# Mixing stage of a hybrid decoder layer: VectorE order, place of the state products, held output tiles, order of the gate products

## The chip, the cores and the metric

The kernel runs on one core of one Trainium2 chip. The metric is the device time of one execution in microseconds (us). The engines are named as in the profile: PE (TensorE), DVE (VectorE), ACT (ScalarE), POOL (GpSimd) and SP (SyncE, which here only issues DMAs); each runs its own instructions in the order of the program, and waits for the others through semaphores.

## The reference

One decoder layer on x of 512 tokens by 1024 channels, in float32: a SwiGLU, a mixing stage, a second SwiGLU, each between RMS norms and with a residual.

```
x = x + 0.5 * post1(swiglu1(pre1(x)))                  # 1024 -> 2*2816 -> 1024
h = pre2(x); q, k, v, u = split(h @ w_mix_in)           # 4 x 512 columns
a = dilated_attention(q, k, v)                          # 8 heads x 64, 3 branches merged: one softmax with a bias
s = s5(u)                                               # 32 groups x 16 channels, 64 complex states, scan over time
s = gelu(s); s = s * sigmoid(s @ w_glu + b_glu)         # 512 x 512
x = x + post2(concat(a, s) @ w_mix_out)                 # 1024 x 1024
x = x + 0.5 * post3(swiglu2(pre3(x)))
```

## The kernel before

Every float32 product is three matmuls on values split in two parts (`mm3`, L129: high by high, high by low, low by high). A weight chunk comes by DMA from SP's queue into `wraw` (one of 3 buffers), ACT casts its high part (`whi`, L102) and DVE or POOL subtracts it from the chunk for the low part (`wlo`, L104). All eight PSUM banks rotate through one pool: the next tile takes a bank whose last reader is done.

`start` (from L216) fetches x and the first weight chunks in four cuts and runs the first two chunks of the first SwiGLU as the cuts arrive; all these DMAs but that of the small parameters (`sw`) are issued by SP.

The stage that the change is about is `mix` (from L843). PE's order in it is written out by hand at its end; `f(n)` advances a generator of filling work by n pieces (`pieces`: half projections of q and k chunks, `prj`, and pieces of the value projection, `prv`), `go(n)` advances the scan on DVE by n steps (`sx`, `Hs`, L1111), and `fg` does both. The order is:

- projection 0 of q, with the late part of the norm hooked in after k-tiles 3 and 7 (`late`); four products `o0` were begun before and are multiplied by the norm into `uT`, go to DRAM (`ud`, L904) and come back in another layout as `um` (L906).
- projection 4 and half of 1, scores of head pair 0, `f(2)`: the rest of 1 and the first half of 5, then `states` (64 matmuls `st` that read `um`; ACT copies the result to `Hs` and `ends`), then the other half of 5, which makes kT of pair 1.
- transposes `pt` of pair 0's probabilities, the value projection with scan steps beside it, scores of pair 1, values `pv` of pair 0, and so on for pairs 1 to 3. Between them lie parts of the output projection (`mo`): `parts` with k-tiles 0 and 1 of several output tiles, each of which holds a PSUM bank until its k-tile 3 is done (12 matmuls for two held tiles before the scores of pair 3).
- the scan's outputs `ys`, the gelu (`ge`, `zg`, split into `zz`), the gate products `gl` of the GLU (48 matmuls: k-tiles 0 to 2 of each of four tiles m, then k-tile 3 of each), output tiles 6 and 7, and the tail of the output projection (`yt`, in the next boundary), which reads the gated result `so`.

`attn_probs` turns one head's scores into probabilities in these steps: for four row blocks, DVE adds the bias and takes the row's extreme (`nm`, L805), ACT takes the Exp with a row sum `den` (L807); then `rd` = 1/`den`, and the four blocks are scaled by it. For pair 0 both last steps are on DVE (L810, L816); for pairs 1 to 3 the reciprocal is a `pow` on POOL (L812) and the scaling on ACT (L818). Instructions given to `fix` keep the order of the program among themselves; others are placed by the scheduler. L805 is not fixed, the scan and the `prj` readers are.

Of the kernel before, what the change touches and what calls it, by code (L numbers as in the profile page):

```python
# [12 lines left out]
ALU = mybir.AluOpType  # L13
# [4 lines left out]
P = 128  # L18
# [22 lines left out]
class Layer:  # L41
# [170 lines left out]
    def start(self, chunks, ipre):  # L212


        nc = self.nc
        self.x = self.ktiles("x")  # L216
        xt = self.a["xT"].rearrange("(k p) t -> p k t", p=P)
        self.xh, self.xl = self.ktiles("xh", F32R), self.ktiles("xl", F32R)
        acc = self.acct()
        cuts = (0, 1, 3, 5, KD)  # L220
        w = [self.wtiles(KD * P) for _ in chunks[:2]]
        nc.sync.dma_start(out=self.x(0), in_=xt[:, 0])
        sw = self.sw
        for a, b in zip(cuts, cuts[1:]):
            for i, t in enumerate(w):
                if a or i:
                    nc.sync.dma_start(out=t[0][:, a * P:b * P], in_=chunks[i][:, a * P:b * P])
                if a and i == 0:
                    nc.sync.dma_start(out=self.x(a), in_=xt[:, a])
            for k in range(a + 1, b):  # L230
                nc.sync.dma_start(out=self.x(k), in_=xt[:, k])
        v = lambda t: t.rearrange("p (k m) -> p k m", m=P)
        o = [self.bank("first") for _ in w]
        for k in range(KD):
            fx = lambda: self.split(self.xh(k), self.xl(k), self.x(k), sw[:, 8 * ipre + k:8 * ipre + k + 1], fix=self.fix)
            if k == 0:
                self.fix(nc.vector.tensor_copy(out=w[0][1][:, :P], in_=sw[:, 52:]))
                fx()
                self.fix(nc.vector.tensor_tensor(out=w[0][2][:, :P], in0=sw[:, 52:],
                                                 in1=w[0][1][:, :P].bitcast(F32), op=ALU.subtract))  # L240
                self.wsplit(*(u[:, :P] for u in w[1]), fix=self.fix)
            else:
                if k in cuts:
                    sl = slice(k * P, cuts[cuts.index(k) + 1] * P)
                    for t in w:
                        self.wsplit(*(u[:, sl] for u in t), fix=self.fix)
                fx()
            for i, (_, hi, lo) in enumerate(w):
                self.mm3(o[i], v(hi)[:, k], v(lo)[:, k], self.xh(k), self.xl(k), k == 0, k == KD - 1)
        self.fix(nc.vector.tensor_copy(out=self.sm, in_=sw[:, :52]))  # L250
        nc.vector.tensor_scalar_mul(self.gh, self.sm, 0.5)
        self.ahead = [self.load(c, (KD, P)) for c in chunks[2:]]
        for k in range(KD):
            self.sq_acc(acc, self.x(k), k == 0, fix=self.fix)
        r4, r = self.rtiles()
        return o, r4, r, self.rstd(acc, r4, r)
# [540 lines left out]
    def attn_probs(self, ap, hp, i, order, place):  # L797
        nc = self.nc
        bias = ap.tile([P, S], F32, name="bias", tag="bias", bufs=2)
        nc.sync.dma_start(out=bias, in_=self.a["bias"][2 * hp + i])  # L800
        sc = ap.tile([P, 1280], F32, name="sc", tag="sc", bufs=2)
        nm, den, rd = (ap.tile([P, 4], F32, name=n, tag=n, bufs=2) for n in ("nm", "den", "rd"))
        for t in order:
            so = sc[:, QOFF[t]:QOFF[t + 1]]
            nc.vector.tensor_tensor_reduce(out=so, in0=place[t], in1=bias[:, 384 - t * P:], scale=1.0,  # L805
                                           scalar=3e38, op0=ALU.add, op1=ALU.min, accum_out=nm[:, t:t + 1])
            nc.scalar.activation(out=so, in_=so, func=AF.Exp, bias=nm[:, t:t + 1], scale=-1.0,  # L807
                                 accum_out=den[:, t:t + 1])
        if hp < 1:
            nc.vector.reciprocal(out=rd, in_=den)  # L810
        else:
            nc.gpsimd.tensor_tensor(out=rd, in0=den, in1=self.mone, op=ALU.pow)  # L812
        for t in range(4):
            so = sc[:, QOFF[t]:QOFF[t + 1]]
            if hp < 1:
                nc.vector.tensor_scalar_mul(so, so, rd[:, t:t + 1])  # L816
            else:
                nc.scalar.activation(out=so, in_=so, func=AF.Copy, scale=rd[:, t:t + 1])  # L818
        return sc
# [26 lines left out]
    def mix(self, first, scope):  # L846
# [3 lines left out]
        nc, a, tc = self.nc, self.a, self.tc  # L850
        dr = self.dr
        xh, xl = self.xh, self.xl
        o0, r4, r, late = first
        ud = dr.tile([4, P, T, NCH], F32, name="ud")

        def proj(c, hooks={}, w=None):

            w = w or self.load(a["wmi"][c], (KD, P))
            o = self.bank("prj")
            for k in range(KD):  # L860
                self.mm3(o, w[0][:, k], w[1][:, k], xh(k), xl(k), k == 0, k == KD - 1)
                if k in hooks:
                    hooks[k]()
                if k == 3 and not hooks:
                    yield
            t = pr[c] = ap.tile([P, S], F32, name="qkT"[c // 4] + "T", tag="qk", bufs=4)
            if c < 4:
                self.fix(nc.vector.scalar_tensor_tensor(out=t, in0=o, scalar=-0.125, in1=r, op0=ALU.mult, op1=ALU.mult))
            else:
                self.fix(nc.vector.tensor_tensor(out=t, in0=o, in1=r, op=ALU.mult))  # L870
            yield
# [20 lines left out]
        for j in range(T):  # L892
            nc.sync.dma_start(out=M[j * 32:(j + 1) * 32, :, j * 32:],
                              in_=self.kd[:, :, :T - j].rearrange("p n d c -> p n (d c)"))
        for _ in proj(0, {3: late[0], 7: late[1]}):
            pass
        w4 = self.load(a["wmi"][4], (KD, P))
        for m in range(4):
# [3 lines left out]
                                    in0=o0[m].rearrange("p (s i j) -> p s i j", j=T, s=SC),  # L902
                                    in1=r.rearrange("p (s i j) -> p s i j", j=T, s=SC), op=ALU.mult)
# [59 lines left out]
        def out_attn(m, ks=range(4)):  # L963

            need(m)
            if m not in mo:
                mo[m] = self.bank("mo")
            o, (wh, wl) = mo[m], wm[m // 2]
            for k in ks:
                i = 4 * (m % 2) + k  # L970
                self.mm3(o, wh[:, i], wl[:, i], cat[:, k], cat[:, 4 + k], k == 0, k == 3)
            if 3 in ks:
                nc.scalar.copy(out=y(m), in_=o)
# [11 lines left out]
        f = lambda n=1: [next(fill, None) for _ in range(n)]  # L985
# [12 lines left out]
        f()  # L998
        sc = scores(0)()
        vn = ap.tile([P, 4, S], F32, name="vn", tag="vn", bufs=1)  # L1000
        f(2)
        for n4 in range(0, NP, 4):
            states(n4)
        f()
        pt = [turn(sc[0]), turn(sc[1])]
        cat = self.b16("cat", F32R)
        scan = self.scan(sx, Hs, ends)
# [1 line left out]
        def go(n=1):  # L1009
            for _ in range(n):  # L1010
                next(scan, None)

        def fg(*n):
            for i in n:
                f()
                go(i)

        def parts(*mk):
            for m, ks in mk:
                out_attn(m, ks)  # L1020
# [8 lines left out]
        pt = [turn(sc[0])]  # L1029
        fg(1)  # L1030
        pt.append(turn(sc[1]))
        fg(1, 2)
        low = values(1, pt)
        go(2)
        low()
        sc = scores(2)()
        fg(2, 1, 1, 1)
        pt = [turn(sc[0]), turn(sc[1])]
        y = self.ktiles("ymix")
        parts((0, (0, 1)), (1, (0, 1)))  # L1040
        go()
        sc = scores(3)
        low = values(2, pt)
        sc = sc()
        go()
        low()
        parts((2, (0, 1)), (3, (0, 1)))
        go()
        parts((0, (2,)), (1, (2,)))
        pt = [turn(sc[0])]  # L1050
        go()
        parts((2, (2,)), (3, (2,)))
        pt.append(turn(sc[1]))
        go()
        out_attn(4, (0, 1))
        low = values(3, pt)
        early.close()
# [6 lines left out]
        zt = self.b16("zz", F32R)  # L1064
        go(9)
        low()
        parts((4, (2,)), (5, range(3)))
        parts(*((m, (3,)) for m in range(6)))
        wg = [[v[:, 4 * m:4 * m + 4] for v in w] for w in (self.load(a["wgl"][m2], (8, P)) for m2 in range(2))
              for m in range(2)]  # L1070
        need(6)
# [9 lines left out]
        so = [st[:, :4], st[:, 4:]]  # L1081
# [3 lines left out]
        def glu(m, ks=range(4)):  # L1085
            if m not in og:
                og[m] = self.bank("gl")
            for k in ks:
                self.mm3(og[m], wg[m][0][:, k], wg[m][1][:, k], zt[:, k], zt[:, 4 + k], k == 0, k == 3)
            if 3 in ks:  # L1090
                t = self.tmp("gt")
                nc.scalar.activation(out=t, in_=og[m], func=AF.Tanh, scale=0.25, bias=self.gh[:, 48 + m:49 + m])
                t2 = self.tmp("go")
                nc.vector.scalar_tensor_tensor(out=t2, in0=t, scalar=1.0, in1=zg[:, m], op0=ALU.add, op1=ALU.mult)
                self.split(so[0][:, m], so[1][:, m], t2, 0.25)

        for m in range(4):
            glu(m, range(3))
        for m in range(4):
            glu(m, (3,))  # L1100
        for m in range(6, KD):
            out_attn(m)
        return y, lambda i: (so[0][:, i], so[1][:, i])
# [137 lines left out]
```

## Time and profile before

| | us |
|---|---|
| median of 3 runs (lowest, highest) | 965.92 (965.55, 967.3) |
| time of the profiled execution | 967.41 |
| its span in the trace | 965.6 |
| PE busy in the span | 944.0 |
| DVE, ACT, POOL busy | 523.9, 372.4, 228.0 |

The granted PE clock averages 0.994 over the profiled span, where 1.00 is 2.4 GHz and 0.50 is 1.2 GHz. Times in the trace count from the start of the span, in us. A matmul of 512 columns shows a duration of 0.39 us, but the next begins 0.227 us after it, since they are pipelined: 12 of them stand in the chain with 2.77 us. The mixing stage lies at about 396 to 564 us. In a view of time a group "x12" is 12 neighbours, and the bracket at the end of a row says how long the engine idled before it and which instruction released it.

### The profile page before, as it was taken

Reading aid. Unit: us, or ns where it says so; the run is one execution under the profiler, and the core shown is the slowest. Engines: PE = TensorE matmul, PEld = TensorE weight load, DVE = VectorE, ACT = ScalarE, POOL = GpSimd, SP = SyncE. Lnnn points to the kernel's source line nnn. Section 1 sums busy time; section 2 is a strip of 40 time slices with the busy share of each in tenths; the row PEclk is TensorE's granted clock in tenths of the full one; section 3 lists DMA queues with packets and bytes.
Section 4 is the critical chain, followed back from the end, with each engine's and each line's share of the span. In section 5 each row is a group of like instructions: output and inputs, shape, how many; then the busy total and the mean of one; then the engine's idle time right before and its main releaser. Section 6 shows DMA issues by size and latency. Waiting matters only on the chain.

```text
span 965.6 us, 12881 instructions
## 1 busy us (share of the span) xinstructions
PE 944.0 (98%) x5082; PEld 789.4 (82%) x5082; DVE 523.9 (54%) x924; ACT 372.4 (39%) x618; POOL 228.0 (24%) x136
## 2 busy tenths in 40 slices
PE   9999999999999999999998999999999999999995
PEld 7888888888888889978766799888888888888884
DVE  7997214453256437667786568655134524444427
ACT  7353324442233224454655554543232312232312
POOL 0334212322133133400000025421122212222300
PEclk9999999999999999999999999999999999999998
DMA  8233333353334240480422430322323223234202
GB/s 264 96 101 115 102 111 129 112 190 93 117 99 144 58 161 24 147 229 23 131 66 76 152 123 1 109 88 88 101 97 109 88 88 109 91 106 131 87 1 88
DMA packets 38173, 102.48 MB, mean 106 GB/s; under 512 B 7616, under 2 KB 10944, under 8 KB 37568
## 3 DMA queue, kind: packets, MB, share of 16 engines
q1 hardware_dynamic: 37104, 98.54, 31.7%
q10 hardware_dynamic: 1008, 3.11, 0.9%
q8 instruction: 40, 0.66, 0.3%
q14 instruction: 21, 0.17, 0.1%
HBM read 94.03 MB, written 7.60 MB: 105 GB/s over the span
## 4 chain that ended last, share of the span: by engine, by line
PE 85%; DVE 6%; ACT 4%; DMA 2%; issue 2%; POOL 1%; SPq 0%; POOLq 0%; ACTq 0%; DVEq 0%
PE gu L129 46%; PE yo L129 20%; PE first L129 6%; PE yt L129 5%; PE prj L129 2%; PE st L129 1%; DVE Hs L1111 1%; PE ys L129 1%; ACT sc L818 1%; DVE sx L1111 1%; DMA um<-ud 1%; ACT sc L807 1%; PE mo L129 1%; ACT whi L102 1%; DVE wlo L104 1%
## 5 line engine op out<-in xcount | busy, mean ns | idle before, releaser
L104 POOL TENSOR_TENSOR wlo<-wraw,whi 128x1024 fp32r<-128x1024 f32 (+2 forms) x62 | 159.0, 2564 | 500.0 <-ACT whi L102 492.5
L102 ACT CAST whi<-wraw 128x1024 fp32r<-128x1024 f32 (+5 forms) x157 | 154.6, 990 | 306.0 <-PE gu L129 123.9
L129 PE MATMUL gu<-xh,whi 128*128 128x512 f32 x656 | 257.6, 393 | 0.0
L129 PE MATMUL gu<-xh,wlo 128*128 128x512 f32 x656 | 255.7, 390 | 0.5 <-DVE wlo L104 0.5
L129 PE MATMUL gu<-xl,whi 128*128 128x512 f32 x656 | 255.3, 389 | 0.0
L104 DVE TENSOR_TENSOR wlo<-wraw,whi 128x1024 fp32r<-128x1024 f32 (+5 forms) x95 | 114.0, 1203 | 122.4 <-ACT whi L102 121.7
L129 PEld LDWEIGHTS gu<-xh,wlo 128*128 128x128 f32 x656 | 123.1, 188 | 26.8 <-DVE wlo L104 1.0
L129 PEld LDWEIGHTS gu<-xh,whi 128*128 128x128 f32 x656 | 123.2, 188 | 25.3 <-issue 0.4
L129 PEld LDWEIGHTS gu<-xl,whi 128*128 128x128 f32 x656 | 123.2, 188 | 25.1
L402 DVE TENSOR_TENSOR ut<-gu,rs 128x512 f32<-128x512 f32 x41 | 28.3, 689 | 103.9 <-PE gu L129 103.8
L149 DVE TENSOR_TENSOR al<-ut,ah 128x512 fp32r<-128x512 f32 x44 | 68.5, 1560 | 24.7 <-ACT ah L148 24.7
L400 DVE TENSOR_TENSOR gt<-gu,rs 128x512 f32<-128x512 f32 x41 | 28.2, 689 | 51.8 <-PE gu L129 51.7
L129 PE MATMUL yo<-ah,whi 128*128 128x512 f32 x144 | 56.0, 389 | 0.0
L129 PE MATMUL yo<-al,whi 128*128 128x512 f32 x144 | 56.0, 389 | 0.0
L129 PE MATMUL yo<-whi,ah 128*128 128x512 f32 x144 | 56.0, 389 | 0.0
L129 PE MATMUL yo<-wlo,ah 128*128 128x512 f32 x144 | 56.0, 389 | 0.0
L129 PE MATMUL yo<-whi,al 128*128 128x512 f32 x144 | 56.0, 389 | 0.0
L129 PE MATMUL yo<-ah,wlo 128*128 128x512 f32 x144 | 56.0, 389 | 0.0
L148 ACT CAST ah<-ut 128x512 fp32r<-128x512 f32 x44 | 27.2, 621 | 61.1 <-DVE ut L403 61.1
L129 PE MATMUL first<-xh,whi 128*128 128x256 f32 (+1 forms) x144 | 43.4, 301 | 0.8 <-ACT xh L151 0.8
L129 PE MATMUL first<-xl,whi 128*128 128x256 f32 (+1 forms) x144 | 42.7, 296 | 0.3 <-DVE xl L152 0.3
L129 PE MATMUL first<-xh,wlo 128*128 128x256 f32 (+1 forms) x144 | 42.4, 295 | 0.0
(194 smaller groups left out, 1408.6 us busy)
## 6 DMA issues: line engine op xcount, KB each, us to landing
wraw<-w2i SPq DMA_DIRECT2D x44, 512.0 KB, 3.5
wraw<-w1i SPq DMA_DIRECT2D x42, 512.0 KB, 3.5
wraw<-w2o SPq DMA_DIRECT2D x18, 512.0 KB, 3.5
wraw<-w1o SPq DMA_DIRECT2D x16, 448.0 KB, 3.4
wraw<-wmi SPq DMA_DIRECT2D x12, 512.0 KB, 3.5
x<-xT SPq DMA_DIRECT2D x8, 256.0 KB, 4.6
w1d<-w1s SPq DMA_DIRECT2D x8, 256.0 KB, 2.7
w2d<-zb SPq DMA_DIRECT2D x2, 1024.0 KB, 4.9
```

The lines of the kernel that those rows point to most:

```text
L102: fix(self.nc.scalar.copy(out=hi, in_=raw))
L104: fix(eng.tensor_tensor(out=lo, in0=raw, in1=hi.bitcast(F32), op=ALU.subtract))
L129: i = self.nc.tensor.matmul(*a, **k)
L148: fix(nc.scalar.copy(out=hi, in_=src))
L149: fix(nc.vector.tensor_tensor(out=lo, in0=src, in1=hi.bitcast(F32), op=ALU.subtract))
L400: nc.vector.tensor_tensor(out=gt, in0=o[f][0], in1=r, op=ALU.mult)
L402: nc.vector.tensor_tensor(out=ut, in0=o[f][1], in1=r, op=ALU.mult)
L807: nc.scalar.activation(out=so, in_=so, func=AF.Exp, bias=nm[:, t:t + 1], scale=-1.0, accum_out=den[:, t:t + 1])
L818: nc.scalar.activation(out=so, in_=so, func=AF.Copy, scale=rd[:, t:t + 1])
L1111: tt = lambda o, x, y, op: self.fix(V.tensor_tensor(out=o, in0=x, in1=y, op=op))
```

## The change

The start: the four DMAs of the second weight chunk go to ACT's queue. In the mixing stage: (1) the norm's late part hangs on k-tiles 1 and 4 of projection 0; (2) both halves of projection 5 come ahead of the state products; (3) L805 is fixed in program order; (4) pair 2's reciprocal and scaling move from POOL and ACT to DVE; (5) before the scores of pair 3, k-tiles 0 and 1 of one output tile are computed (6 matmuls) where two were (12); tiles 1 to 3 follow the values of pair 2; (6) k-tiles 2 and 3 of output tile 5 move from before the scan's outputs to behind the gate products; (7) the gate products run k-tile by k-tile over all four tiles, with a bank for each. Scan steps (`go`) are dealt out differently between the pieces.

```diff
@@ start
-                    nc.sync.dma_start(out=t[0][:, a * P:b * P], in_=chunks[i][:, a * P:b * P])
+                    (nc.scalar if i else nc.sync).dma_start(out=t[0][:, a * P:b * P], in_=chunks[i][:, a * P:b * P])
@@ attn_probs
-            nc.vector.tensor_tensor_reduce(out=so, in0=place[t], ...
+            self.fix(nc.vector.tensor_tensor_reduce(out=so, in0=place[t], ...
-        if hp < 1:
+        if hp % 2 == 0:
             nc.vector.reciprocal(out=rd, in_=den)
...
-            if hp < 1:
+            if hp % 2 == 0:
                 nc.vector.tensor_scalar_mul(so, so, rd[:, t:t + 1])
@@ mix
-        for _ in proj(0, {3: late[0], 7: late[1]}):
+        for _ in proj(0, {1: late[0], 4: late[1]}):
...
-        f(2)
+        f(3)
         for n4 in range(0, NP, 4):
             states(n4)
-        f()
         pt = [turn(sc[0]), turn(sc[1])]
...
-        fg(1, 2)
+        fg(4, 3)
         low = values(1, pt)
-        go(2)
+        go()
         low()
         sc = scores(2)()
-        fg(2, 1, 1, 1)
+        fg(1, 1, 1, 1)
         pt = [turn(sc[0]), turn(sc[1])]
         y = self.ktiles("ymix")
-        parts((0, (0, 1)), (1, (0, 1)))
-        go()
+        out_attn(0, (0, 1))
         sc = scores(3)
         low = values(2, pt)
         sc = sc()
         go()
         low()
-        parts((2, (0, 1)), (3, (0, 1)))
+        parts((1, (0, 1)), (2, (0, 1)), (3, (0, 1)))
...
-        parts((4, (2,)), (5, range(3)))
-        parts(*((m, (3,)) for m in range(6)))
+        parts((4, (2,)), (5, (0, 1)))
+        parts(*((m, (3,)) for m in range(5)))
...
-        for m in range(4):
-            glu(m, range(3))
-        for m in range(4):
-            glu(m, (3,))
+        for k in range(4):
+            for m in range(4):
+                glu(m, (k,))
+        out_attn(5, (2, 3))
```

In the printed orders the line numbers of the changed kernel lie one or two off those of before. PE around the state products (`prj` is projection 5, `st` the states), before:

```order
L129 MATMUL prj<-xl,whi 128x512
L129 MATMUL prj<-xh,wlo 128x512
L129 MATMUL st<-um,w_3541 128x128 x32
L129 MATMUL prj<-xh,whi 128x512
L129 MATMUL prj<-xl,whi 128x512
```

And in the changed kernel (`pt` are pair 0's transposes, `prv` the value projection):

```order
L129 MATMUL prj<-xl,whi 128x512
L129 MATMUL prj<-xh,wlo 128x512
L129 MATMUL st<-um,w_3541 128x128 x32
L832 MATMUL pt<-ident,sc 128x128 x20
L129 MATMUL prv<-whi,xh 128x512
```

The second half of projection 5 (12 matmuls) has moved from behind the states to ahead of them.

PE around the scores of pair 3 (`sc`) and the values of pair 2 (`pv`), before:

```order
L129 MATMUL mo<-cat,whi 128x512 x2
L129 MATMUL mo<-cat,wlo 128x512
L129 MATMUL mo<-cat,whi 128x512 x2
L129 MATMUL mo<-cat,wlo 128x512
L129 MATMUL sc<-kT,qT 128x512 x2
L129 MATMUL sc<-kT,qT 128x128 x2
L129 MATMUL sc<-kT,qT 128x384 x2
L129 MATMUL sc<-kT,qT 128x256 x2
L129 MATMUL pv<-ptt,vn 64x512 x2
```

And in the changed kernel, from the transposes of pair 2 on:

```order
L832 MATMUL pt<-ident,sc 128x128 x20
L129 MATMUL mo<-cat,whi 128x512 x2
L129 MATMUL mo<-cat,wlo 128x512
L129 MATMUL mo<-cat,whi 128x512 x2
L129 MATMUL mo<-cat,wlo 128x512
L129 MATMUL sc<-kT,qT 128x512 x2
L129 MATMUL sc<-kT,qT 128x128 x2
L129 MATMUL sc<-kT,qT 128x384 x2
L129 MATMUL sc<-kT,qT 128x256 x2
L129 MATMUL pv<-ptt,vn 64x512 x2
```

Half of the `mo` matmuls between the transposes and the scores are gone from there; `pv` still follows the scores directly.

DVE between the readers of pair 3's q and k projections (`qT`, `kT`; `sx` and `Hs` are scan steps), before:

```order
L868 SCALAR_TENSOR_TENSOR qT<-prj,rs 128x512
L1111 TENSOR_TENSOR sx<-pw,Hs 128x480 x2
L1111 TENSOR_TENSOR Hs<-Hs,sx 128x4x120
L104 TENSOR_TENSOR wlo<-wraw,whi 128x1024
L1111 TENSOR_TENSOR Hs<-Hs,sx 128x4x120
L1111 TENSOR_TENSOR sx<-pw,Hs 128x480 x2
L1111 TENSOR_TENSOR Hs<-Hs,sx 128x4x120 x2
L870 TENSOR_TENSOR kT<-prj,rs 128x512
```

And in the changed kernel, from the scaling (L817) of pair 2's second head on, which stands behind that `qT`:

```order
L811 RECIPROCAL rd<-den 128x4
L1109 TENSOR_TENSOR Hs<-Hs,sx 128x4x120
L817 TENSOR_SCALAR sc<-sc,rd 128x128
L817 TENSOR_SCALAR sc<-sc,rd 128x256
L817 TENSOR_SCALAR sc<-sc,rd 128x384
L817 TENSOR_SCALAR sc<-sc,rd 128x512
L1109 TENSOR_TENSOR Hs<-Hs,sx 128x4x120
L1109 TENSOR_TENSOR sx<-pw,Hs 128x480 x2
L1109 TENSOR_TENSOR Hs<-Hs,sx 128x4x120
L104 TENSOR_TENSOR wlo<-wraw,whi 128x1024
L1109 TENSOR_TENSOR Hs<-Hs,sx 128x4x120
L871 TENSOR_TENSOR kT<-prj,rs 128x512
```

The reciprocals and scalings of both heads of pair 2 now stand in DVE's queue ahead of `kT`.

## Rows read from the trace of the kernel before

**Rows 1.** The page: busy time and share of the span, each engine.

```profile
PE 944.0 (98%) x5082; PEld 789.4 (82%) x5082; DVE 523.9 (54%) x924; ACT 372.4 (39%) x618; POOL 228.0 (24%) x136
```

**Rows 2.** Waits of PE: us in total, times, longest.

```profile
PE pv L129 <- DVE nm L805: 3.3, 1, 3.3
PE st L129 <- DMA um<-ud: 1.9, 1, 1.9
...
PE first L129 <- ACT xh L151: 0.8, 1, 0.8
PE sc L129 <- DVE kT L870: 0.7, 1, 0.7
PE gl L129 <- DVE zz L149: 0.6, 2, 0.4
PE yt L129 <- DVE so L152: 0.6, 1, 0.6
```

**Rows 3.** Stretches: length, busy by PE, PEld, DVE, ACT, POOL, PE's granted clock, DMA.

```profile
427.80:431.40 3.60, 3.60 (x18) 3.60 (x19) 1.55 (x2) 0.79 (x3) 0.00 (x0) 0.54 0.93 320
431.40:436.80 5.40, 5.40 (x49) 5.40 (x48) 0.00 (x0) 3.74 (x12) 0.00 (x0) 0.99 0.13 51
...
509.40:514.00 4.60, 4.60 (x19) 2.21 (x20) 4.60 (x18) 3.46 (x12) 0.96 (x1) 0.63 0.00 0
...
544.00:548.00 4.00, 2.55 (x9) 1.27 (x9) 3.23 (x6) 3.46 (x7) 0.00 (x0) 1.00 0.01 4
```

**Rows 4.** The chain that ended last: start, us, what.

```profile
418.53 9.11 DMA um<-ud
427.78 9.01 PE st L129 x64
...
472.93 2.77 PE prj L129 x12
```

**Rows 5.** DVE in order of time: scan steps and projection readers (start, us).

```profile
441.63 0.76 DVE L1111 TENSOR_TENSOR sx<-pw,Hs 128x256 f32<-128x256 f32 x2
...
482.31 0.69 DVE L870 TENSOR_TENSOR kT<-prj,rs 128x512 f32<-128x512 f32 x1 [3.03 <-PE prj L129]
...
484.86 0.34 DVE L1111 TENSOR_TENSOR sx<-pw,Hs 128x32 f32<-128x32 f32 x2
485.12 0.52 DVE L1111 TENSOR_TENSOR Hs<-Hs,sx 128x32 f32<-128x32 f32 x3
...
498.82 1.23 DVE L104 TENSOR_TENSOR wlo<-wraw,whi 128x1024 fp32r<-128x1024 f32 x1 [3.79 <-ACT whi L102]
...
500.53 1.22 DVE L1111 TENSOR_TENSOR sx<-pw,Hs 128x480 f32<-128x480 f32 x2
501.67 1.34 DVE L1111 TENSOR_TENSOR Hs<-Hs,sx 128x480 f32<-128x480 f32 x2
502.93 0.68 DVE L870 TENSOR_TENSOR kT<-prj,rs 128x512 f32<-128x512 f32 x1
```

**Rows 6.** DVE: reciprocal and scaling of one head of pair 0.

```profile
426.13 0.18 DVE L810 RECIPROCAL rd<-den 128x4 f32<-128x4 f32 x1 [0.69 <-ACT sc L807]
426.34 1.28 DVE L816 TENSOR_SCALAR sc<-sc,rd 128x128 f32<-128x128 f32 x4
```

**Rows 7.** PE: pair 2's transposes, pair 3's scores, pair 2's values.

```profile
497.88 2.35 PE L831 MATMUL pt<-ident,sc 128*128 128x128 f32 x20
...
503.67 2.43 PE L129 MATMUL sc<-kT,qT 64*128 64x512 f32 x16 [0.68 <-DVE kT L870]
509.39 2.02 PE L129 MATMUL pv<-ptt,vn 128*64 128x512 f32 x6 [3.29 <-DVE nm L805]
```

**Rows 8.** POOL in order of time, beside the gate products.

```profile
558.23 2.52 POOL L104 TENSOR_TENSOR wlo<-wraw,whi 128x1024 fp32r<-128x1024 f32 x1 [39.50 <-ACT whi L102]
```

**Rows 9.** DVE in order of time, the same stretch.

```profile
557.79 0.69 DVE L1094 SCALAR_TENSOR_TENSOR go<-gt,zg 128x512 f32<-128x512 f32 x1
558.76 2.52 DVE L1094 SCALAR_TENSOR_TENSOR go<-gt,zg 128x512 f32<-128x512 f32 x1 [0.28 <-ACT gt L1092]
```

More of the change, by code (lines that the diff above doesn't have):

```diff
@@ L804, in attn_probs @@
             so = sc[:, QOFF[t]:QOFF[t + 1]]
-            nc.vector.tensor_tensor_reduce(out=so, in0=place[t], in1=bias[:, 384 - t * P:], scale=1.0,
-                                           scalar=3e38, op0=ALU.add, op1=ALU.min, accum_out=nm[:, t:t + 1])
+            self.fix(nc.vector.tensor_tensor_reduce(out=so, in0=place[t], in1=bias[:, 384 - t * P:], scale=1.0,
+                                                    scalar=3e38, op0=ALU.add, op1=ALU.min,
+                                                    accum_out=nm[:, t:t + 1]))
             nc.scalar.activation(out=so, in_=so, func=AF.Exp, bias=nm[:, t:t + 1], scale=-1.0,
                                  accum_out=den[:, t:t + 1])
-        if hp < 1:
+        if hp % 2 == 0:
             nc.vector.reciprocal(out=rd, in_=den)
@@ L1053, in mix @@
         pt.append(turn(sc[1]))
-        go()
         out_attn(4, (0, 1))
```

## The prediction

> **What bounds the kernel now.** I read the page first: PE is busy for 944.0 of 965.6 us [rows 1], so only what keeps PE waiting, or slow, can move the end. The waits of PE name the places [rows 2]: 3.3 us where pair 2's values wait for the first score of pair 3 to leave PSUM, 1.9 us where the states wait for the DMA of `um`, 0.7 us before pair 3's scores, 0.6 us for `zz` in the gate products, 0.6 us for `so` in the tail, 0.8 us at the start. The stretches around the two long waits then show a second loss [rows 3]: after the 1.9 us wait the granted clock is 0.54 for 3.60 us, and after the 3.3 us one 0.63 for 4.60 us, so between the 1.2 and 2.4 GHz levels; it is 0.99 in the stretch that follows the first. The short waits beside the gate products left it at 1.00. Last I read DVE and PE in order of time, to see what comes late once a wait is gone [rows 5, 7].
>
> **Term A, the states.** The 12 matmuls put ahead of them last 2.77 us [rows 4]. PE stopped for `um` 1.93 us before 427.78, at 425.85, so it now reaches the states at 428.6. The last `um` landed at 418.53 + 9.11 = 427.64 [rows 4]: even a transfer that is no earlier comes in time. It should be earlier: the norm's late part hangs three k-tiles sooner (9 matmuls, 9 x 0.227 = 2.0 us), `uT` comes ahead of `qT` on DVE, and SP issues the four `ud` ahead of two weight loads that stood ahead of them; a `wmv` load and the four `um` follow. I estimate 425.5, 3 us to spare. So the 1.93 us go, with the low clock behind them: 18 matmuls took 3.60 us, where 49 took 5.40 in the next stretch, 0.110 each [rows 3], so 3.60 - 18 x 0.110 = 1.62. A is worth 1.93 + 1.62 = 3.55. The scan's first step (441.63 [rows 5]) waits for ACT's copies of the states, and moves with them; three casts of weights now stand among these copies on ACT. That no step moves would make A worth 0; I take 3.5, since PE reaches the value projection that much earlier and the casts' data lands well before.
>
> **Pinning L805** costs nothing for pair 0: PE has two half projections ahead of the first reader of its probabilities, and the scaling of its second head ended at 427.6 [rows 6] with the transposes due behind the states, after 435. Bounds: 0 to half a microsecond of scaling delay, which that slack covers.
>
> **Term B, pairs 2 and 3.** In DVE's queue, kT of pair 2 to kT of pair 3 took from 483.0 to 503.6 [rows 5], 20.6 us, of which 3.8 us were idle before `wlo` (waiting for ACT, which was busy with the scaling that now leaves it). So 16.8 us are work. Added are two reciprocals with four scalings each, 2 x (0.18 + 1.28) = 2.9 [rows 6], and two large scan steps that now lie there, each 2.4 us from 500.53 to 502.93 [rows 5]: 4.8. Three small ones leave, each 0.34 + 0.52, some 0.8 us with their overlap: -2.4. Sum 22.1 us. With A, the count begins at 479.5 and kT of pair 3 ends at 501.6, 2.0 earlier than before.
> PE gets there sooner. The transposes of pair 2 may start at 497.88 - 3.5 = 494.4, and they, with 2.35 us [rows 7], and 6 `mo` matmuls (1.37) would be done at 498.1. So PE now waits 3.5 us, part before the second head's transposes (its scaling ends some 4.7 us ahead of kT, at 496.9: scan steps, a `wlo` and kT itself lie between), the rest before the scores. The new waits take the place of the 0.68 us one.
> Behind the scores the 3.3 us wait goes: with one held tile less, `pv` is given a bank whose last reader is kT of pair 3, which the scores have waited for anyway. So `pv` begins at 501.6 + 2.43 = 504.0, not 509.39 [rows 7]: 5.4 earlier. Then 6 `mo` matmuls come that stood ahead before (-1.4), the clock stays up (4.60 x 0.37 = +1.7), and about 0.5 more wait for `cat` and pair 3's scaling is left than before. Pair 3's values are thus 5.2 earlier, of which 3.5 is A: B is worth 1.7. No row shows these waits together, so its bounds: -0.5 if the two new waits lower the clock as the 3.3 us one did (1.7 lost) and half a microsecond of copies is late, and 6.1 if DVE comes in time: 3.3 + 0.7 + 1.7 and 0.4 of small waits.
>
> **Term C, the gate products.** In 544 to 548 PE ran 9 matmuls in 4.00 us [rows 3], and 9 x 0.227 = 2.04, so 1.96 us are lost to `zz`. By k-tiles over four tiles, each `zz` has 12 matmuls, 2.77 us, before the next is needed, while before PE needed three of them within one tile. I take 2.0; bounds 0 and 2.1.
>
> **Term D, the tail.** `yt` waited 0.6 us for `so` [rows 2]. 30 `mo` matmuls instead of 24 stand between the gate products and `yt`, 1.4 us more, so the wait should go: 0.6. What can eat this is POOL's `wlo`, 2.52 us from 558.23, beside which a `go` of 0.69 us took 2.52 and ended with it [rows 8, 9]. This pair of operations stays in the program; if it falls on the last `go`, which now come close together, up to 1.6 us are late. Bounds -1.0 and 0.6. The Trainium skill ("SBUF — State Buffer", section "SBUF: two separate sides") says that DVE operations with two SBUF inputs and GpSimd share a pair of ports by an exclusive lock, and the loser waits for the whole instruction. The trace agrees: by its rule the `go` is held to the end of POOL's instruction and not merely slowed, which is the lower bound of D: the sum would be 1.6 lower, at 959.7, within the forecast's own range.
>
> **The start.** Second-chunk weights on ACT's queue let SP issue x sooner, but ACT's first cast of x now waits behind four issues. PE's 0.8 us wait for the second x tile [rows 2] hangs on a weight cast ahead of it on ACT. No row shows ACT issuing here; bounds -0.5 and 0.3, and I take 0. The order of small operations on DVE in the first SwiGLU changes too, all with PE busy: 0.
>
> **Sum.** 3.5 + 1.7 + 2.0 + 0.6 = 7.8. The profiled execution took 967.41 us (its span 965.6 and 1.8 around it), 1.49 above the median of 965.92. 967.41 - 7.8 = 959.6, and beside the median 958.1 us.
>
> **Rivals.**
> 1. DVE is later than counted, and PE's clock falls at the new waits (B = -0.5, D = -0.4). For it: 22 us of DVE work in line, and both long waits of before lowered the clock. Against: the new wait is in two pieces with transposes between. 3.5 - 0.5 + 2.0 - 0.4 = 4.6: 961.3.
> 2. DVE comes in time, and the old waits go with no new ones (B = 6.1): 3.5 + 6.1 + 2.0 + 0.6 = 12.2: 953.7. For it: ACT is relieved of two scalings. Against: the count of DVE's queue.
> 3. The change does not do what it says at the states: ACT's casts hold the copies of the states, the scan starts no earlier, A = 0 and B = 0 as PE waits for the chain at pair 1 instead; C stays and D is lost to POOL (-1.0). 2.0 - 1.0 = 1.0: 964.9.
> 4. Slower: the clock. PE waits at the second head's transposes, at the scores, for `cat` and for pair 3's scaling, all from 495 to 515. If the clock stays low through them, at the 0.63 of before [rows 3], until PE is free of waits near 526, 30 us lose 0.37 each, 11 us against the 7.8: 3.3 slower, 969.2. It decides from 21 us of low clock on (7.8 / 0.37). Against: after each of the two waits of before it was back within 3.6 and 4.6 us [rows 3].
>
> **How the numbers follow.** The forecast has 0.52, rival 1 0.22, rival 2 0.14, rival 3 0.07, rival 4 0.05. The forecast's own range is 955.5 to 960.5. The range takes in rival 1 with a little more for the start's bound, and most of the way to rival 2: 954.0 to 963.0. What a measurement can tell from no change is 0.2%, 1.9 us: faster (forecast, rivals 1 and 2) 0.88, within it (rival 3) 0.07, slower (rival 4) 0.05.
>
> **What would show it.** A: no wait of `st` for `um` and a clock near 1.00 there; the first scan step near 438. B: a wait of `sc` for kT of some 2 us and one of `pt` for the scaling of 1.4, and none of `pv` for `nm`; kT of pair 3 at about 501 and `pv` at 504. C: no waits of `gl`. D: `yt` without a wait, unless a `go` of 2.5 us lies beside POOL's `wlo`. I am wrong if PE waits before the scores for less than 1 us (rival 2), or if the clock around 500 to 515 is under 0.9 (rivals 1 and 4).

## The result and the profile after

The changed kernel takes 960.24 us (median of 4 runs, 959.66 to 962.07), the kernel before beside it 966.61: ratio 0.9937, 95% interval 0.9918 to 0.9956. Measured again in six runs beside the kernel before it took 959.96, ratio 0.9923 (0.9909 to 0.9937). The prediction had 958.1, between 954.0 and 963.0, and faster. The profiled execution took 959.66, 7.75 under the profiled one of before (967.41); the sum had 7.8.

The waits of PE in the changed kernel (us in total, times, longest), against [rows 2]:

```profile
PE sc L129 <- DVE kT L871: 2.3, 1, 2.3
...
PE first L129 <- DVE xl L152: 0.6, 2, 0.3
...
PE first L129 <- ACT xh L151: 0.4, 1, 0.4
PE mo L129 <- DVE cat L996: 0.3, 1, 0.3
PE yt L129 <- DVE so L152: 0.3, 1, 0.3
PE pt L832 <- ACT sc L819: 0.3, 1, 0.3
```

The waits of `pv`, `st` and `gl` are gone; one new long wait stands before pair 3's scores. The stretches (columns as in [rows 3]) show that PE's clock, 0.54 and 0.63 there, is full behind the states and around pair 2's values:

```profile
427.80:431.40 3.60, 3.60 (x27) 3.33 (x26) 2.24 (x12) 2.93 (x11) 0.00 (x0) 1.00 0.85 304
498.90:501.20 2.30, 0.03 (x1) 0.00 (x0) 2.30 (x4) 0.00 (x0) 0.00 (x0) 1.00 0.10 32
501.20:505.20 4.00, 3.97 (x26) 2.13 (x28) 4.00 (x8) 0.81 (x2) 0.00 (x0) 1.00 0.30 113
537.20:541.20 4.00, 4.00 (x19) 3.30 (x18) 3.18 (x7) 3.37 (x7) 0.00 (x0) 1.00 0.02 4
```

The last is the head of the gate products: 19 matmuls in 4 us, where before it were 9. DVE in order of time, against [rows 5] and [rows 6]:

```profile
438.02 0.76 DVE L1109 TENSOR_TENSOR sx<-pw,Hs 128x256 f32<-128x256 f32 x2
...
478.91 0.69 DVE L871 TENSOR_TENSOR kT<-prj,rs 128x512 f32<-128x512 f32 x1 [0.59 <-PE prj L129]
...
495.24 1.27 DVE L817 TENSOR_SCALAR sc<-sc,rd 128x128 f32<-128x128 f32 x4
...
500.40 0.68 DVE L871 TENSOR_TENSOR kT<-prj,rs 128x512 f32<-128x512 f32 x1
501.00 1.22 DVE L1109 TENSOR_TENSOR sx<-pw,Hs 128x480 f32<-128x480 f32 x2
502.13 0.65 DVE L1109 TENSOR_TENSOR Hs<-Hs,sx 128x480 f32<-128x480 f32 x1
502.70 0.68 DVE L805 CUSTOM_DVE_ANT_0 sc<-sc,bias 128x512 f32<-128x512 f32 x1
...
503.31 0.65 DVE L1109 TENSOR_TENSOR Hs<-Hs,sx 128x480 f32<-128x480 f32 x1
503.88 1.22 DVE L104 TENSOR_TENSOR wlo<-wraw,whi 128x1024 fp32r<-128x1024 f32 x1
```

And PE, against [rows 7]:

```profile
429.30 7.30 PE L129 MATMUL st<-um,w 128*128 128x128 f32 x64
...
501.23 2.43 PE L129 MATMUL sc<-kT,qT 64*128 64x512 f32 x16 [2.30 <-DVE kT L871]
503.59 2.37 PE L129 MATMUL pv<-ptt,vn 128*64 128x512 f32 x16
```

Note that 2.3 us lie between kT and L805, the first reading of a score, from start to start. Before it were 5.7, from 502.93 [rows 5] to 508.64:

```profile
503.53 1.22 DVE L1111 TENSOR_TENSOR sx<-pw,Hs 128x480 f32<-128x480 f32 x2
504.67 0.65 DVE L1111 TENSOR_TENSOR Hs<-Hs,sx 128x480 f32<-128x480 f32 x1
505.24 1.22 DVE L104 TENSOR_TENSOR wlo<-wraw,whi 128x1024 fp32r<-128x1024 f32 x1
506.37 0.65 DVE L1111 TENSOR_TENSOR Hs<-Hs,sx 128x480 f32<-128x480 f32 x1
506.94 1.22 DVE L1111 TENSOR_TENSOR sx<-pw,Hs 128x480 f32<-128x480 f32 x2
508.07 0.65 DVE L1111 TENSOR_TENSOR Hs<-Hs,sx 128x480 f32<-128x480 f32 x1
508.64 0.69 DVE L805 CUSTOM_DVE_ANT_0 sc<-sc,bias 128x512 f32<-128x512 f32 x1
```

Of these, the `wlo` and the `Hs` behind it (1.7 us) come after L805 in the changed kernel; the second `sx` with its `Hs` (1.7 us) is no longer there.

### The profile page after: what moved, and what is told of

Same layout as the page of the kernel before. It is cut to its first block, busy times and chain, and to the rows that moved or that the text cites. A ratio compares the mean times of both kernels' runs of the same rounds, so it can differ in the third digit from the quotient of the medians.

```text
span 957.9 us, 12872 instructions
## 1 busy us (share of the span) xinstructions
PE 940.9 (98%) x5082; PEld 787.8 (82%) x5082; DVE 526.3 (55%) x934; ACT 367.6 (38%) x610; POOL 224.2 (23%) x134
## 4 chain that ended last, share of the span: by engine, by line
PE 88%; DVE 6%; ACT 2%; issue 1%; DMA 1%; POOL 0%; SPq 0%; POOLq 0%; DVEq 0%; ACTq 0%
PE gu L129 45%; PE yo L129 20%; PE yt L129 6%; PE first L129 5%; PE prj L129 3%; PE prv L129 2%; DVE wlo L104 1%; PE st L129 1%; PE ys L129 1%; PE gl L129 1%; DMA wraw<-w1i 1%; PE mo L129 1%; DVE Hs L1109 1%; DVE sx L1109 1%; PE pt L832 1%
## 5 line engine op out<-in xcount | busy, mean ns | idle before, releaser
L104 DVE TENSOR_TENSOR wlo<-wraw,whi 128x1024 fp32r<-128x1024 f32 (+5 forms) x95 | 116.0, 1226 | 121.8 <-ACT whi L102 121.5
```

The source lines that it names most:

```text
L104: fix(eng.tensor_tensor(out=lo, in0=raw, in1=hi.bitcast(F32), op=ALU.subtract))
```

## The experiments

Each ran in five rounds beside the kernel before, in three groups of four. "The changed kernel" in the comparisons is the base, which ran in the first group only, with two held tiles, the start and less DVE work ahead of kT. Both L805 runs and both runs on the states are the second group, the others the third. The kernel before took 967.08, 966.50 and 966.65 us in the three groups, so a difference to the base across groups is uncertain by about half a microsecond beside the spread of the runs; the ratios are taken within a group. The base is the first run:

> The changed kernel once more, as the base of this group: 959.5 to 961.5 us, ratio to the kernel before 0.992 to 0.995.

It gave the 959.96 us told above.

**Two held tiles again.**

```diff
-        out_attn(0, (0, 1))
+        parts((0, (0, 1)), (1, (0, 1)))
         sc = scores(3)
...
-        parts((1, (0, 1)), (2, (0, 1)), (3, (0, 1)))
+        parts((2, (0, 1)), (3, (0, 1)))
```

> The changed kernel with two held output tiles (12 mo matmuls) ahead of pair 3's scores again. Theory of the prediction (the bank that pv gets is what freed it): pv is given the bank of the first score of pair 3 again and waits for nm some 3 us, with the clock down behind it; 3 to 5 us above the changed kernel. Rival (the pinned order of L805 freed it: that first score is now read first, at about 503.3, before the scan steps): pv hardly waits, under 0.3 us, and the 6 mo matmuls fill 1.4 us of the 2.3 us wait for kT; 0.5 to 1.4 us under the changed kernel.

960.05 us, ratio 0.9924 (0.9911 to 0.9938): no change. `pv` did not wait. PE's waits:

```profile
PE sc L129 <- DVE kT L871: 0.9, 1, 0.9
PE mo L129 <- DVE cat L996: 0.8, 1, 0.8
PE mo L129 <- ACT cat L995: 0.6, 1, 0.6
```

The 6 `mo` matmuls fill 1.4 us of the wait before the scores, and the waits for `cat` behind the values grow from 0.3 to 1.4 us. So the prediction's reason for the freed `pv`, one held tile less, is not needed.

**L805 not fixed; and both undone.** The diff of the first:

```diff
-            self.fix(nc.vector.tensor_tensor_reduce(...))
+            nc.vector.tensor_tensor_reduce(...)
```

> The changed kernel with L805 not fixed in program order; one tile held as in it. Theory A (bank: with one held tile pv's bank is last read by kT, whatever the order of L805): pv does not wait for nm, the time is within 1 us of the changed kernel. Theory B (the pinned order is what freed pv): pv waits for nm 2 to 3 us, and the time is 2 to 4 us above the changed kernel.

961.81 us, ratio 0.9945 (0.9929 to 0.9961); `pv` did not wait for `nm`, but the scores waited 4.0 us for kT, and the clock was 0.66 from 501.7 to 505.3, behind that wait: theory A's sign, though not its time. The second has both diffs:

> The changed kernel with both undone: two tiles held ahead of pair 3's scores, and L805 not fixed. Each of the two frees pv alone (theory C, from the run with two held tiles and pinned L805, whose pv did not wait): with both undone pv has a bank of pair 3's scores that is read behind scan steps, waits for nm 2 to 3.5 us, and the time is 2 to 4 us above the changed kernel. Rival D (neither mattered; the wait went since DVE's whole queue is shorter there): no wait, within 1 us of the changed kernel.

960.34 us, ratio 0.9934 (0.9918 to 0.9949): rival D. DVE there:

```profile
502.09 0.68 DVE L871 TENSOR_TENSOR kT<-prj,rs 128x512 f32<-128x512 f32 x1
502.69 1.22 DVE L1109 TENSOR_TENSOR sx<-pw,Hs 128x480 f32<-128x480 f32 x2
503.83 0.65 DVE L1109 TENSOR_TENSOR Hs<-Hs,sx 128x480 f32<-128x480 f32 x1
504.40 0.68 DVE L805 CUSTOM_DVE_ANT_0 sc<-sc,bias 128x512 f32<-128x512 f32 x1
```

Neither the held tile nor the pin freed `pv`. Common to the changed kernel, to this one and to the run with two held tiles is that the first score is read 2.3 us after kT. In the changed kernel that reading ends at 503.38, before `pv` begins at 503.59: even the bank of the first score would not have held it up.

**The dealing of scan steps alone, on the kernel before.**

```diff
-        fg(1, 2)
+        fg(4, 3)
         low = values(1, pt)
-        go(2)
+        go()
         low()
         sc = scores(2)()
-        fg(2, 1, 1, 1)
+        fg(1, 1, 1, 1)
...
         parts((0, (0, 1)), (1, (0, 1)))
-        go()
         sc = scores(3)
...
         pt.append(turn(sc[1]))
-        go()
         out_attn(4, (0, 1))
```

> The kernel before with one part of the change alone: scan steps are dealt out earlier (fg(4, 3) and one go at pair 1's values, fg(1, 1, 1, 1) behind pair 2's scores, no go between the mo tiles and the scores of pair 3); two held tiles, L805 not fixed, pair 2's scaling on POOL and ACT, states and gate products as before. Theory A (new: what freed pv is that less DVE work lies between kT of pair 3 and its first score, 3.4 us in place of 5.7, with the bank as it was): pv waits for nm about 1 us in place of 3.3, the clock stays up behind it, and the time is 2 to 4 us under the kernel before. Rival (the bank or the pin is needed for it): pv waits 3 us or more, within 1 us of the kernel before.

964.63 us, ratio 0.9973 (0.9961 to 0.9986), 2.0 under the kernel before; the profiled run, 964.60, showed this on DVE and PE:

```profile
502.42 0.69 DVE L870 TENSOR_TENSOR kT<-prj,rs 128x512 f32<-128x512 f32 x1
503.02 1.22 DVE L1109 TENSOR_TENSOR sx<-pw,Hs 128x480 f32<-128x480 f32 x2
504.16 0.65 DVE L1109 TENSOR_TENSOR Hs<-Hs,sx 128x480 f32<-128x480 f32 x1
504.73 1.22 DVE L104 TENSOR_TENSOR wlo<-wraw,whi 128x1024 fp32r<-128x1024 f32 x1
505.86 0.65 DVE L1109 TENSOR_TENSOR Hs<-Hs,sx 128x480 f32<-128x480 f32 x1
506.43 0.68 DVE L805 CUSTOM_DVE_ANT_0 sc<-sc,bias 128x512 f32<-128x512 f32 x1
```

```profile
504.19 2.43 PE L129 MATMUL sc<-kT,qT 64*128 64x512 f32 x16
507.18 1.08 PE L129 MATMUL pv<-ptt,vn 128*64 128x512 f32 x4 [0.55 <-DVE nm L805]
```

With 4.0 us between kT and L805, `pv` waits 0.55 us and not 3.29, though it still waits for the first score's reading, so for that bank. Theory A holds: what bounded `pv` was the DVE work queued between kT and the reading of the scores. The dealing alone takes one scan step (1.7 us) out of there. The `wlo` and half a step that also stand behind L805 in the changed kernel still stand ahead of it here; what moves them is not isolated, as the runs with two held tiles, with L805 free, with both, and with pair 2's scaling on ACT all have them behind it (2.3 us from kT to L805 in each).

**The states.**

```diff
-        f(3)
+        f(2)
         for n4 in range(0, NP, 4):
             states(n4)
+        f()
```

> The changed kernel with the states ahead of the second half of projection 5 again, the norm's late part as in the changed kernel. Theory A (the reorder is what removed the wait for um and the low clock behind it, term A of the prediction): st waits over 1.5 us for um, clock near 0.55 behind it, and the time is 2.5 to 3.5 us above the changed kernel. Theory B (um, which landed at 427.0 in the changed kernel, would be in time by the earlier late part almost alone): PE reaches the states at 426.7, waits 0.3 to 0.6 us, the clock stays, and the time is 0 to 0.6 us above.

961.60 us, ratio 0.9947 (0.9929 to 0.9964), 1.6 above the changed kernel, with overlapping intervals of the ratios: between the theories. The profiled execution was the slowest of the six (963.91), 1.0 us later than the changed kernel's already at 50 us. In it the last `um` landed at 428.64 (the profile names a `wmv` load beside it as the releaser), `st` waited 1.33 us and the clock stayed:

```profile
429.00:432.60 3.60, 3.60 (x32) 3.60 (x33) 2.24 (x11) 2.57 (x9) 0.00 (x0) 1.00 0.80 292
```

With the norm's late part put back as well (`{3: late[0], 7: late[1]}`):

> The changed kernel with both undone: the states ahead of the second half of projection 5, and the norm's late part on k-tiles 3 and 7. Both theories: st waits 1.5 to 2 us for um again and the clock falls behind it; the values of pair 0 are 3.5 us later. Theory A (the delay reaches the end, as the prediction's sum has it): 3 to 3.5 us above the changed kernel. Rival (DVE's queue ahead of pair 3's kT had taken it up in part): 1 to 2 us above.

966.76 us, ratio 0.9993 (0.9978 to 1.0007), 6.8 above the changed kernel, but its runs spread from 963.53 to 968.77, and the profiled one, 963.86, is 4.2 above the changed kernel's. `st` waited 2.13 us, and behind it:

```profile
428.40:432.00 3.60, 3.60 (x21) 3.60 (x22) 2.32 (x7) 1.71 (x6) 0.00 (x0) 0.63 0.92 335
```

Both parts together are worth 4 us and more, and in the profiled execution nothing of it was taken up later (4.05 us behind pair 0's values, 4.2 at the end). What makes the other runs up to 5 us longer than the profiled one is open: only that one has a trace.

**The gate products in the old order.**

```diff
-        for k in range(4):
-            for m in range(4):
-                glu(m, (k,))
+        for m in range(4):
+            glu(m, range(3))
+        for m in range(4):
+            glu(m, (3,))
```

> The changed kernel with the gate products in the old order (k-tiles 0 to 2 of each tile, then k-tile 3 of each). Term C of the prediction: gl waits for zz again, some 2 us in all, and the time is 1.7 to 2.1 us above the changed kernel. Rival (the tail waits for POOL and DVE anyway, so a part is taken back at yt): 0 to 1 us above, with the yt wait gone.

963.34 us, ratio 0.9965 (0.9953 to 0.9977), 3.4 above the changed kernel, more than either expected. `gl` waits 1.4 us for `zz`, and then:

```profile
536.60:540.60 4.00, 2.54 (x12) 1.17 (x8) 3.19 (x6) 3.30 (x7) 0.00 (x0) 1.00 0.02 4
540.60:544.60 4.00, 4.00 (x11) 3.14 (x12) 3.73 (x4) 2.82 (x3) 0.00 (x0) 0.57 0.16 45
```

After the same short waits that left the clock at 1.00 before [rows 3] it was 0.57 here over 4 us, which cost 1.7 (4.0 x 0.43).

**The start.** All weight DMAs on SP's queue again (`nc.sync.dma_start(...)`):

> The changed kernel with all weight DMAs of the start on SP's queue again. Theory A: the 0.8 us that the changed kernel is behind at 36 us come from ACT's queue at the start alone (first cast of x at 5.2 instead of 4.0 us, and the norm's pow late at 35 us as its consequence): the lag is 0 at 36 us and the time 0.8 us under the changed kernel. Theory B: the part at 35 us (0.5 us) comes from other small operations that moved: the lag stays at 0.4 to 0.5 us, and the time is 0.3 us under.

959.12 us, ratio 0.9914 (0.99 to 0.9929), 0.84 under the changed kernel: theory A, by the trace above all, as the intervals of the ratios overlap: PE is within 0.05 us of the kernel before at 36 us, where the changed kernel is 0.8 behind it (0.4 of it by 33 us, the rest at the norm at 35 us). In the changed kernel ACT begins its first cast of x at 5.17 us, here at 3.97. The norm's `pow` on POOL, for which PE waits at 35 us, comes 3.5 us later in the changed kernel, behind DVE's work on the parameters of the `s5` part (`pp`). The changed kernel, then this one:

```profile
34.13 1.03 POOL L192 TENSOR_TENSOR r<-nv,mhalf 128x4 f32<-128x4 f32 x1 [7.44 <-DVE pp L633]
```

```profile
30.66 1.04 POOL L192 TENSOR_TENSOR r<-nv,mhalf 128x4 f32<-128x4 f32 x1 [4.32 <-DVE nv L190]
```

The size varies between executions: at 50 us PE is 0.35 to 1.8 us behind the kernel before's trace in the ten traces with ACT issuing, and 0.04 to 0.4 in the three others with SP issuing.

**Pair 2's scaling on POOL and ACT again** (`if hp < 1:` in both places).

> The changed kernel with pair 2's reciprocal and scaling on POOL and ACT again. Theory A (the sum of DVE's queue decides when kT of pair 3 is made, as in the prediction): 2.9 us less in it, kT at 497.5 in place of 500.4, the wait before the scores goes, 1.5 to 2.5 us under the changed kernel. Theory B (ACT takes it over: its cast of the next weight chunk stands behind the scaling, and DVE's subtraction and kT behind that cast): kT at 500 or later, the second head's transposes at 497 or later, within 0.7 us of the changed kernel or above it.

958.35 us, ratio 0.9915 (0.9903 to 0.9928): 1.6 under the changed kernel's median, 0.8 by the ratios, whose intervals overlap. The rows show both theories at work, kT 0.75 earlier and the transposes held by ACT:

```profile
494.53 1.23 DVE L104 TENSOR_TENSOR wlo<-wraw,whi 128x1024 fp32r<-128x1024 f32 x1 [0.51 <-ACT whi L102]
...
499.65 0.68 DVE L871 TENSOR_TENSOR kT<-prj,rs 128x512 f32<-128x512 f32 x1
```

```profile
494.92 1.92 ACT L819 ACTIVATE sc<-sc,rd 128x128 f32<-128x128 f32 x4 [0.42 <-POOL rd L813]
```

PE waited 1.2 us before the scores and 0.5 us at the transposes. Moving the scaling to DVE is no gain that these runs show; whether it costs anything is not told apart.

**Less DVE work ahead of kT, and the best version.**

```diff
         sc = scores(2)()
-        fg(1, 1, 1, 1)
+        fg(1, 0, 0, 1)
```

> The changed kernel with two of the four large scan steps between pair 2's and pair 3's kT dealt out behind that kT (fg(1, 0, 0, 1) after the scores of pair 2). Theory A: what PE waits for before pair 3's scores is DVE's queue alone, so 4.8 us less in it brings kT from 500.4 to about 495.6, the 2.3 us wait goes to under 0.5, and the time is 2.0 to 3.0 us under the changed kernel, since DVE has idle time behind the scan. Theory B: the scan's end becomes the wait: ys waits for it, or pair 3's values for low parts behind it, and the time is within 0.7 us of the changed kernel.

958.19 us, ratio 0.9901 (0.9884 to 0.9918): 1.8 under the changed kernel, the slowest of its four runs (958.39) under the fastest of the base's six (959.30), though the ratios' intervals overlap. kT stood at 496.62, and the wait before the scores was gone. With the start's DMAs on SP too:

> The changed kernel with the two gains found so far: two scan steps dealt out behind pair 3's kT (1.8 us under it when run alone) and the start's weight DMAs on SP's queue (0.8 us under it alone). If they add, as the places lie far apart: 957.3 us, 2.6 under the changed kernel, ratio to the kernel before 0.989. Rival (the start's lag is given back at a later wait): as the first alone, 958.2.

955.85 us, ratio 0.9891 (0.9877 to 0.9906), 4.1 under the changed kernel and the fastest here. In medians that is 1.5 below the sum of the two, but across groups; by the ratios the two add, with 0.9892 expected (0.0022 and 0.0009 below the base's 0.9923). Beside the 1.2 us before PE's first instruction, no wait over 0.6 us is left:

```profile
PE first L129 <- ACT xh L151: 0.6, 1, 0.6
PE gu L129 <- DVE wlo L104: 0.5, 1, 0.5
PE prj L129 <- DVE wlo L104: 0.5, 1, 0.5
...
```

## Why the prediction came out

PE's instructions of the two traces are set side by side; each term is how much earlier PE got over its stretch.

- **Start: 0 predicted, -0.8 measured**, outside its bounds (-0.5 to 0.3). ACT's issues, which the step counted, cost 0.4 in these traces; the moved parameter work on DVE, put at 0, made the norm late at 35 us and cost the other 0.4. Putting the DMAs back removes both.
- **A: 3.5 predicted, 4.2 measured** (0.8 later before the states, 3.4 earlier behind pair 0's values). Right in mechanism: no wait, full clock. The estimate that `um` lands at 425.5 failed: it landed at 427.0, since its transfers, though issued earlier, ran beside the weight loads as before. Undoing the reorder alone brought back 1.3 us of wait and raised the median by 1.6 (not clear of the intervals); undoing the earlier late part with it brought back the low clock and cost 4.2 between traces. So a good part of A is the earlier late part, which the prediction took for a reserve.
- **Pinning L805: 0 predicted**; without it the median is 1.9 us higher, but the ratios' intervals overlap. Not told apart.
- **B: 1.7 predicted, 2.0 measured** (3.4 earlier behind pair 0's values, 5.4 behind pair 3's transposes). The count of DVE's queue was right: 22.1 us from kT to kT, 21.5 measured (479.60 to 501.08), kT done at 501.1 where 501.6 was said, `pv` at 503.6 where it was 504.0. The wait before the scores is 2.3 us (2.0 expected), that of the transposes some 0.7 in small pieces (1.4 expected). The step that failed is the reason for the freed `pv`: "with one held tile less, `pv` is given a bank whose last reader is kT". With two tiles held, and with L805 free besides, it is as free. What counted was the DVE work between kT and the first reading of a score, which went from 5.7 to 2.3 us. The dealing of scan steps alone made it 4.0, and the wait 0.55; why the other 1.7 us (`wlo` and half a step) came behind the reading is open. Two more scan steps now stand ahead of kT, and with pair 2's scaling they make the new wait. The two waits of before, 0.68 and 3.29, thus became one of 2.3.
- **C: 2.0 predicted, 2.3 measured** (the gate products' own stretch). Undoing it cost 3.4, as the clock fell in that run.
- **D: 0.6 predicted, 0.4 measured.** POOL's `wlo` met a `go` again, the second of four in [rows 8, 9] and now the last, as the prediction's lower bound feared; `yt` waits 0.3 all the same (POOL, then DVE):

```profile
552.75 2.41 POOL L104 TENSOR_TENSOR wlo<-wraw,whi 128x1024 fp32r<-128x1024 f32 x1 [39.41 <-ACT whi L102]
```

```profile
553.29 2.41 DVE L1092 SCALAR_TENSOR_TENSOR go<-gt,zg 128x512 f32<-128x512 f32 x1 [0.40 <-ACT gt L1090]
```

`go` ends 0.54 us after POOL's instruction does (555.16), a little under the 0.69 us that it takes by itself. In [rows 8, 9] it is 0.53 us after, not "with it" as the prediction read. The Trainium skill's rule ("SBUF — State Buffer", section "SBUF: two separate sides") would have it so: held by the other's lock, then run.
- The sum: -0.8 + 4.2 + 2.0 + 2.3 + 0.4 = 8.1, of which the end of the span gives 0.3 back; 7.75 measured between the two executions, 6.4 between the medians (7.1 when measured again). That 7.8 came within 0.1 is in part luck: the start's loss and A's surplus cancel, and of the two executions the one before was 1.5 above its median and the one after the fastest of its four, with a full clock before pair 3's scores. The median, 960.24, is 2.1 above the 958.1 forecast.
- Rival 1 is half true: behind the new wait the clock was low in some executions, in the base run 0.58:

```profile
501.10:505.10 4.00, 4.00 (x16) 2.25 (x16) 3.48 (x7) 0.81 (x2) 0.00 (x0) 0.58 0.30 115
```

Over 500 to 515 it averages 0.89 there, just under the 0.9 that the prediction gave as a sign of being wrong, and 1.00 in the first trace. There pair 2's values were 1.5 us later than in the first trace, and the scan's outputs only 0.5, since the waits for `cat` and for pair 3's scaling (0.34 and 0.26 us in the first trace) were gone. Rival 2's time was not reached by this change, but `fg(1, 0, 0, 1)` shows that its condition can be made.

## What to carry to other kernels

When a product waits for an accumulator to be read, count the work in the reader's queue between the event that starts the product and that reading, before looking at which bank it gets; and work that is moved out of there goes somewhere, so count the wait ahead as well. Cost the instructions that a scheduler moves along with an edit (here the parameters' work in the first 35 us), not only those that the diff names. Undo each part alone: here three (the start, the held tile, pair 2's scaling) brought no gain that can be shown, and two scan steps dealt out later brought 1.8 us more.

## What the hardware showed that was not expected

- PE's clock fell after some waits and not after others of the same length. In six traces the scores of pair 3 waited 2.29 to 2.31 us for kT: the changed kernel's two, and those that undid the states, the states with the late part, the gate products' order, and the start. In three of them the clock stayed at 1.00 over the next 4 us (the changed kernel's first, the states with the late part, the gate products); in the other three it was 0.57 or 0.58 over 4 us that began within 1.3 us of the first score. After 2.63 us it stayed at 1.00 in the run with both undone. A clock forecast from a wait's length alone was a coin toss here, worth up to 1.7 us.
- What such a fall costs depends on what follows. Before pair 3's scores most was absorbed by later waits (of 1.5 us, 0.5 were left at the scan's outputs). Among the gate products, with no wait behind that could shrink, the run in the old order ended its gate products 3.4 us later than the changed kernel and its span 3.3 us later.
